# The end of FF2 in a one-layer hybrid decoder step: preloaded residual, a last step in row groups, a norm moved into the next stage

## The chip, the cores and the metric

The kernel runs on one core of one Trainium2 chip. The metric is the device time of one execution in microseconds. PE is the matrix engine, DVE the vector engine, ACT the scalar engine, POOL the general-purpose engine, SP the engine that only issues transfers. PSUM is the memory with eight banks that products are summed in.

## The reference

One layer of a decoder is applied to a prompt of 2048 tokens and to 8 x 4 sampled tokens, with a model width of 1024. Two branches (a gated recurrence and windowed attention) are merged, and an MLP with squared ReLU follows. The part that matters here is the end:

```python
x = x + m @ w_o
h2 = _rmsnorm(x, n2)
x = x + jnp.square(jax.nn.relu(h2 @ w_ff1)) @ w_ff2      # FF1: 1024 -> 4096, FF2: 4096 -> 1024
y = _rmsnorm(x, normf_w)
```

All in float32. `_rmsnorm` divides each token's row by the root of its mean square plus 1e-6 and multiplies by a weight.

## The kernel before

**Layout.** Activations are stored transposed: 128 channels on the partitions, tokens along the free axis. A matrix of 1024 channels is eight tiles (`KD = 8`). The tokens are worked in two superblocks (`sb` 0 and 1) of 1024 and 1056 tokens, each in two halves (`o` 0 and 1) of `Th` = 512 and 528 tokens. In superblock 1 a half doesn't fit one PSUM bank, and is worked in two chunks of 264.

**Products.** Every float32 value is split into a high part, rounded for the fast product format, and a remainder: ACT copies the high part (`split_in`, `split_out`, lines 145 and 249) and DVE subtracts it (lines 146 and 250). A product is then three matmuls: high x high, high x low, low x high (lines 257 to 259 and 1396 to 1398).

**Strassen.** FF1 and FF2 are each done as a 2 x 2 block product by Winograd's form of Strassen, with seven products instead of eight. The blocks are halves of the tokens and halves of the channels. Operands called A11, A12, A22 are blocks, and S1 to S4 are sums of blocks; B.. and T1 to T4 are the same for weights. S operands of FF1 lie in DRAM (`sd`), and so do the operands of FF2, which FF1 writes at its end of each unit (`us`, line 1301, from POOL's queue).

**FF1** (`strassen_T`, `Unit`, `Wpair`) runs in units of one channel tile and one chunk. A unit's part `a` needs only A11, A12 and early weights: two products of 12 matmuls (fB and fC). Six (superblock 0) or ten (superblock 1) units do `a` ahead, with a hook `early(i)` after each, in which the splits of the S operands are done. Then each unit runs `b` (three products) and the unit before it `c` (two products; its last one needs S4).

**FF2** runs the seven steps of the list `steps` one after another. A step takes four groups `g` of 512 of the 4096 channels. For each `g` it loads the operand (`u_load`, line 1351) and two weight blocks (`w2_blk`, line 1335), both from SP's queue, and does 48 products (x 2 chunks) into four PSUM banks, `j` = 0 to 3. After the last `g`, each bank is added to the output blocks that the step belongs to (`evac`, line 1404 for a copy by ACT and line 1406 for an addition by DVE). `yacc` holds the outputs: 16 tiles, eight per half.

The **last step** (A22 x T4) is written out differently. All four groups' operands are loaded first, and the output channels are taken in two pairs (`jp`); for each pair all four groups' weights are held, and each bank runs over all groups before the next begins.

**The final norm** is the class `Fin` inside FF2. `load` brings the residual `x1d` from DRAM (line 1369, SP's queue). `add` adds it to the output (DVE, line 1373), squares it (ACT, line 1374) and sums the squares over channel tiles (POOL, or DVE in the last blocks, line 1378). `end` transposes the sums on PE (line 207), sums on DVE (208), forms the power -1/2 on POOL (210), and spreads the row back over the partitions by transposes on PE (219) and an ACT copy (220). `out` multiplies by weight and norm row (ACT line 1389 and POOL line 1390, or one DVE instruction, line 1387, in the very last tiles) and stores the tile. The first half (`f0`) is normed among the last step's products; the second half (`f1`; two chunks in superblock 1) after them.

**Order.** The code hands instructions to a planner that gives each engine a fixed sequence. The program's order is the priority, and an instruction may move ahead of earlier ones that the planner, by its own costs, thinks not ready. On the chip each engine runs its sequence in order. The lists `todo` and `hooks` decide where in the program order the side work stands: one or two entries are taken after each group of products. The transfers of one issuing engine go out in the order of its sequence too. SRAM tiles of one stage reuse the addresses of earlier stages' tiles and wait for those to be released; `op(slot, ...)` gives seven long-lived slots.

## Time and profile before

| | |
|---|---|
| median of three runs | 2945.36 us (2944.08 to 2948.93) |
| the profiled execution's time | 2943.06 us |
| its span, first to last instruction | 2941.3 us |
| busy share of the span | PE 95%, DVE 60%, ACT 39%, POOL 18% |
| mean granted PE clock | 0.981 |
| first FF2's last step | from 2154.7 us of the span |
| second FF1's first products | from 2211.5 us |
| second FF2's last step, last product | 2856.5, 2926.8 us |

A profile row names a line of the kernel, an engine, the operation and its tiles. "[2.99 <-POOL xo]" behind a row is the time for which the engine stood idle before it, and what ended that. A row of the waits gives the total, the number and the longest. Numbers in tile names are left out, so `f` is any PSUM bank of FF2, `fB_f` and `fC_f` are banks of FF1, `n_y` and `rb_y` are the norm's transposes, and `hw2T`, `lw2T` are the split weights of a T step.

### The profile page before, as it was taken

How to read it: one execution, taken by the hardware profiler on the slowest of the kernel's cores; microseconds unless marked ns; L12 is line 12 of the kernel's file. 1: busy time of each engine (PE TensorE's matmuls, PEld its weight loads, DVE VectorE, ACT ScalarE, POOL GpSimd, SP SyncE). 2: the span in 40 equal slices, each digit the busy share in tenths (PEclk: the TensorE clock that was granted, in tenths of full speed). 3: DMA queues.
4: the chain of work that ended last, by engine and by line, in shares of the span. 5: the costliest groups of instructions: out<-in, count | busy, mean ns of one | idle time of the engine just before them, and what ended most of it. 6: DMA issues, size and time to landing. Idle time of an engine off the chain costs nothing.

```text
span 2941.3 us, 50086 instructions
## 1 busy us (share of the span) xinstructions
PE 2797.4 (95%) x20053; PEld 2438.8 (83%) x20053; DVE 1776.3 (60%) x2785; ACT 1145.0 (39%) x2148; POOL 535.4 (18%) x797
## 2 busy tenths in 40 slices
PE   7999999999999999999999999999986999999996
PEld 5778887787799867777798888778876999999996
DVE  4574645746765367436666877754567777654464
ACT  4442345323444434334333333444443333344342
POOL 0100211102200112320122222100043343300003
PEclk9999999999999999989999999999998999999998
DMA  5227562377633435523355544785555444565553
GB/s 179 74 82 255 192 195 64 96 242 259 222 124 110 131 117 190 172 74 103 107 171 196 183 152 143 262 304 181 200 169 183 156 157 138 168 242 187 192 183 96
DMA packets 347897, 488.81 MB, mean 166 GB/s; under 512 B 22528, under 2 KB 224080, under 8 KB 347648
## 3 DMA queue, kind: packets, MB, share of 16 engines
q1 hardware_dynamic: 295536, 340.84, 37.0%
q0 software_dynamic: 39584, 129.18, 11.9%
q10 hardware_dynamic: 12544, 15.60, 1.5%
q8 instruction: 157, 2.57, 0.4%
...
## 4 chain that ended last, share of the span: by engine, by line
PE 77%; DMA 7%; issue 5%; DVE 5%; POOL 3%; ACT 2%; SPq 0%; DVEq 0%; ACTq 0%; POOLq 0%
PE f L1396 7%; PE f L1397 7%; PE f L1398 7%; PE fB_f L257 3%; PE fB_f L259 3%; PE fB_f L258 3%; PE fD_f L257 2%; PE fD_f L259 2%; PE fD_f L258 2%; PE ps_hgb L159 1%; PE ps_hgb L160 1%; PE wob L1236 1%; PE wob L1234 1%; PE fB_z L257 1%; PE wob L1235 1%
## 5 line engine op out<-in xcount | busy, mean ns | idle before, releaser
L1396 PE MATMUL f<-f2S,hw2T 128*128 128x264 f32 (+1 forms) x576 | 183.6, 319 | 0.0
L1397 PE MATMUL f<-f2S,hw2T 128*128 128x264 f32 (+1 forms) x576 | 183.5, 319 | 0.0
L1398 PE MATMUL f<-f2S,lw2T 128*128 128x264 f32 (+1 forms) x576 | 183.4, 318 | 0.0
L146 DVE TENSOR_TENSOR lw2T<-lw2T,hw2T 128x1024 fp32r<-128x1024 f32 x64 | 83.3, 1304 | 100.2 <-ACT hw2T L145 99.3
L257 PE MATMUL fB_f<-S,w1T_f 128*128 128x264 f32 (+1 forms) x384 | 123.4, 322 | 9.2 <-ACT p_f L320 5.7
L1378 POOL TENSOR_TENSOR xo<-xo 128x512 f32<-128x512 f32 (+2 forms) x25 | 34.3, 1372 | 492.5 <-ACT xo L1374 484.7
L1396 PE MATMUL f<-f2A,h_w2B 128*128 128x264 f32 (+1 forms) x384 | 122.4, 319 | 0.0
L258 PE MATMUL fB_f<-S,w1T_f 128*128 128x264 f32 (+1 forms) x384 | 122.4, 319 | 0.0
L1397 PE MATMUL f<-f2A,h_w2B 128*128 128x264 f32 (+1 forms) x384 | 122.3, 319 | 0.0
L1398 PE MATMUL f<-f2A,l_w2B 128*128 128x264 f32 (+1 forms) x384 | 122.3, 318 | 0.0
L259 PE MATMUL fB_f<-S,w1T_f 128*128 128x264 f32 (+1 forms) x384 | 122.2, 319 | 0.0
L145 ACT CAST hw2T<-lw2T 128x1024 fp32r<-128x1024 f32 x64 | 67.3, 1051 | 134.1 <-DMA lw2T<-w_T 129.9
L1236 PE MATMUL wob<-m_b,l_wob 128*128 128x512 f32 (+2 forms) x320 | 112.3, 352 | 5.3 <-DVE l_wob L250 5.3
L1234 PE MATMUL wob<-m_b,h_wob 128*128 128x512 f32 (+2 forms) x320 | 113.5, 355 | 3.9 <-DVE ga_b L1122 2.8
L1396 PEld LDWEIGHTS f<-f2S,hw2T 128*128 128x128 f32 x576 | 108.4, 188 | 7.5
L1397 PEld LDWEIGHTS f<-f2S,hw2T 128*128 128x128 f32 x576 | 108.4, 188 | 7.4
L1398 PEld LDWEIGHTS f<-f2S,lw2T 128*128 128x128 f32 x576 | 108.0, 188 | 7.5
L1235 PE MATMUL wob<-m_b,h_wob 128*128 128x512 f32 (+2 forms) x320 | 112.5, 352 | 0.0
L146 DVE TENSOR_TENSOR f2S<-f2S 128x1024 fp32r<-128x1024 f32 (+1 forms) x64 | 79.7, 1254 | 48.7 <-ACT f2S L145 48.1
L250 DVE TENSOR_TENSOR l_w2B<-rw2B,h_w2B 128x1024 fp32r<-128x1024 f32 x48 | 58.7, 1224 | 81.8 <-ACT h_w2B L249 72.5
L249 ACT CAST w1T_f<-w1r_f 128x512 fp32r<-128x512 f32 x128 | 77.3, 619 | 79.2 <-DVE w1r_f L293 37.8
L250 DVE TENSOR_TENSOR w1T_f<-w1r_f,w1T_f 128x512 fp32r<-128x512 f32 x128 | 90.1, 710 | 25.8 <-ACT w1T_f L249 25.6
...
## 6 DMA issues: line engine op xcount, KB each, us to landing
...
f2S<-u_S SPq DMA_DIRECT2D x32, 528.0 KB
...
```

Of the source, the lines that this page charges most:

```text
L146: nc.vector.tensor_tensor(lo, F(lo), F(hi), ALU.subtract)
L249: nc.scalar.copy(dh, src)
L250: nc.vector.tensor_tensor(dl, src, F(dh), ALU.subtract)
L257: nc.tensor.matmul(ps, wh, ah, start=(first and k == 0), stop=False, skip_group_check=not first)
L258: nc.tensor.matmul(ps, wh, al, start=False, stop=False, skip_group_check=not first)
L259: nc.tensor.matmul(ps, wl, ah, start=False, stop=(last and k == 3), skip_group_check=not first)
L1234: nc.tensor.matmul(p, wh, ah, start=(k == 0), stop=False)
L1235: nc.tensor.matmul(p, wh, al, start=False, stop=False)
L1236: nc.tensor.matmul(p, wl, ah, start=False, stop=(k == KD - 1))
L1396: nc.tensor.matmul(ps, wh, ah, start=first, stop=False, skip_group_check=cont)
L1397: nc.tensor.matmul(ps, wh, al, start=False, stop=False, skip_group_check=cont)
L1398: nc.tensor.matmul(ps, wl, ah, start=False, stop=lastk, skip_group_check=cont)
```

## The change

- **Residual preload.** In steps 0 to 3 of FF2, after the first group, the residual is loaded from POOL's queue straight into the four output tiles that the step writes first. Every evacuation is then an addition on DVE; the ACT copies, the residual loads on SP's queue and the additions of line 1373 are gone.
- **Last step of superblock 0 by row groups.** It runs in the same loop as the other six. After each of its groups the slot of that group takes the next FF1 operand (S2, S1, S3, A22; loads from POOL's queue); S2 and S1 are split before the stage ends, S3 and A22 in the hooks of FF1.
- **Second half's norm of superblock 0 in the next FF1.** Its output tiles lie in slot 6. Squares, statistics, spread and stores are in the hooks after the first nine units. S4, which needs slot 6, is loaded after the tenth and split in `mid`, after the first `b`.
- **POOL.** The sums of squares and the scalings are DVE instructions. POOL keeps the power and the issue of transfers.
- In superblock 1 the last step keeps its order with two channel pairs; statistics and spread of each norm are entries of their own, some products apart, and the first chunk's norm of the second half is among the last products.
- In the first FF1, the three operand loads stand after unit 0 and their splits after units 3 and 4. Under the w_o product ahead of superblock 1's first stage, the norm of the next tokens is done two channel tiles at a time instead of four.

```diff
                 def fin1(k0, o=o, rbz=rbz, xr=xr):
-                    for k in range(k0, k0 + 4):
+                    for k in range(k0, k0 + 2):
                         norm_x(xr[:, k], k, rbz)
                         if o == 0:
                             split_k(hT_next, k, xr[:, k])
@@ -1220,7 +1225,8 @@
                 half.append((loads, lambda o=o, rbz=rbz: spread(rbz, stats[f"z{o}"].rs, Tn, f"z{o}"), fin1))
             (ld0, rb0_, fin0), (ld1, rb1_, fin1_) = half
-            todo += [ld0, rb0_, lambda: [ld1(), fin0(0)], lambda: [rb1_(), fin0(4)], lambda: fin1_(0), lambda: fin1_(4)]
+            todo += [lambda: [ld0(), rb0_()], lambda: [ld1(), rb1_(), fin0(0)]] + [lambda k=k: fin0(k) for k in (2, 4, 6)]
+            todo += [lambda: [fin1_(0), fin1_(2)], lambda: fin1_(4), lambda: fin1_(6)]
         n2 = Norm(wk_tmp, T, n2c, f"f{B}")
         rings = (sw_ps, mm_ps, hg_ps)
         for n in range(0, KD, 2):
...
+    class Fin:
+        def __init__(f, c0, ln, y, x, ns, q, ring=tp_ps):
+            f.ring, f.c0, f.ln, f.y, f.x, f.ns, f.q, f.acc, f.N = ring, c0, ln, y, x, ns, q, None, f"y{c0}"
+        def sq(f, *js):
+            for j in js:
+                x = f.x("acc" if f.acc is None else "sq")
+                nc.scalar.activation(x, f.y(j), AF.Square)
+                if f.acc is None:
+                    f.acc = x
+                else:
+                    tt(f.acc, f.acc, x, ALU.add)
+        def stat(f):
+            f.rs = f.ns(f"rs_{f.N}")[0:WT[f.ln], 0:f.ln // WT[f.ln]]
+            stat(f.rs, f.acc, f.ln, f.N, f.ring)
+        def spread(f):
+            f.rb = f.x("rb")
+            spread(f.rb, f.rs, f.ln, f.N, f.ring)
+        def out(f, *js):
+            for j in js:
+                y = f.y(j)
+                nc.vector.scalar_tensor_tensor(y, y, nfc[:, j:j + 1], f.rb, ALU.mult, ALU.mult)
+                f.q.dma_start(yT[j * P:(j + 1) * P, f.c0:f.c0 + f.ln], y)
+    f1 = None
     for sb in range(nsb):
         smp, ns, T, segs, halves, tiles = geometry(2 * sb + 1)
         ns2 = ns // 2
         us = {o: [tc.dram_tile([4 * P, Th], F32, name=f"u_{o}_{g}_{sb}") for g in range(KG)] for o in OPS}
         with tc.tile_pool(name=f"f1_{sb}", bufs=1, reuse_waits="tile") as fp:
-            hooks = []
-            for nm, slot in (("S3", 2), ("A22", 3), ("S4", 6)) if sb == 0 else (("S2", 4), ("S1", 5), ("S3", 2), ("A22", 3), ("S4", 6)):
-                ff_ops[nm] = v = opv(slot, nm)
-                hooks += op_load(sb, v, *ff_src(sb, nm), now=False)
+            def get(nm, slot):
+                ff_ops[nm] = opv(slot, nm)
+                return op_load(sb, ff_ops[nm], *ff_src(sb, nm), now=False)
+            if sb == 0:
+                ready = []
+                def split_some():
+                    for _ in range(3):
+                        if ready:
+                            ready.pop(0)()
+                hooks = [[lambda: ready.extend(get("S3", 2) + get("A22", 3) + get("S4", 6))], [], [], [split_some], [split_some], []]
+            else:
+                f1.x = lambda r: fp.tile([P, f1.ln], F32, tag="fa" if r == "acc" else "fs", name=f"fx_{r}")
+                f1.ns = lambda name: fp.tile([P, 8], F32, tag="ns", name=name)
+                hooks = [[lambda: f1.sq(0, 1, 2, 3)], [lambda: f1.sq(4, 5, 6, 7)], late_ops[0:2], [f1.stat], late_ops[2:4], [f1.spread], [lambda: f1.out(0, 1, 2)],
+                         [lambda: f1.out(3, 4, 5)], [lambda: f1.out(6, 7)], [lambda: s4_load.extend(get("S4", 6))]]
+            s4_load = []
             def early(i):
-                for _ in range(2 if i >= (3 if sb == 0 else 4) else 0):
-                    if hooks:
-                        hooks.pop(0)()
+                for f in hooks[i]:
+                    f()
...
         slots = iter([0, 1] + [2, 3, 4, 5] * 8)
         with tc.tile_pool(name=f"f2_{sb}", bufs=1, reuse_waits="tile") as fp:
-            yacc = [[fp.tile([P, Th], F32, tag=f"y{o}{j}", name=f"y{o}{j}_{sb}") for j in range(KD)] for o in range(2)]
-            def y_tmp(tag, name):
+            if last:
+                y1, xo = None, raw8(6, Th, f"xo{sb}")
+            else:
+                y1, xo = raw8(6, Th, f"y1_{sb}"), fp.tile([P, 6, Ths[sb + 1]], F32, name=f"xo{sb}")
+            yacc = [[y1[:, j] if o and not last else fp.tile([P, Th], F32, tag=f"y{o}{j}", name=f"y{o}{j}_{sb}") for j in range(KD)] for o in range(2)]
+            def f2_ns(name):
                 return fp.tile([P, 8], F32, tag="ns", bufs=2, name=name)
+            def fin_of(o, t0, ln, regs, q):
+                regs, n = dict(regs), [0]
+                def x(r):
+                    if r == "sq":
+                        n[0] += 1
+                        r = f"sq{n[0] % 2}"
+                    return xo[:, regs[r], t0:t0 + ln]
+                return Fin(off[sb] + o * Th + t0, ln, lambda j: yacc[o][j][:, t0:t0 + ln], x, f2_ns, q)
...
             def evac(si, j, t0, ln, ps):
                 c11, c12, c21, c22 = (yacc[o][4 * h + j][:, t0:t0 + ln] for o in range(2) for h in range(2))
-                sets, adds = (((c11,), ()), ((c22,), ()), ((c12,), ()), ((c21,), (c22,)), ((), (c11,)), ((), (c12, c22, c21)), ((), (c21,)))[si]
-                for o in sets:
-                    nc.scalar.copy(o, ps)
-                for o in adds:
+                for o in ((c11,), (c22,), (c12,), (c21, c22), (c11,), (c12, c22, c21), (c21,))[si]:
                     tt(o, ps, o, ALU.add)
-            f0 = Fin(0, 0, Th, {**{j: j for j in range(KD)}, "rb": 1})
-            cut = Th // 2 if last else Th
-            f1 = [Fin(1, t0, ln, {4: 2, 5: 3, 6: 4, 7: 5, 0: 6, 1: 7, 2: 3, 3: 4, "rb": 5})
-                  for t0, ln in (((0, cut), (cut, Th - cut)) if last else ((0, Th),))]
+            f0 = fin_of(0, 0, Th, {"acc": 0, "sq0": 1, "sq1": 2, "rb": 3}, nc.gpsimd)
+            cut = Th // 2
+            f1s = [fin_of(1, t0, cut, {"acc": 4, "sq0": 5, "sq1": 6, "rb": 7}, nc.sync) for t0 in (0, cut)]
+            if not last:
+                f1 = Fin(off[sb] + Th, Th, lambda j, y1=y1: y1[:, j], None, None, nc.gpsimd, hg_ps)
+            n_si = 6 if last else 7
             todo = []
-            for si, (ao, wo) in enumerate(steps[:6]):
+            for si, (ao, wo) in enumerate(steps[:n_si]):
                 if fresh[si]:
                     banks = [[rings[si][j](f"f2_{sb}_{si}_{j}_{t0}")[:, 0:ln] for (t0, ln) in chunks] for j in range(4)]
                 if si == 1 and not last:
                     nv = [opT(sb + 1, g, f"A1{g}") for g in range(2)]
-                    rr = raw8(6, Ths[sb + 1], f"fr{sb + 1}")
-                    todo = [lambda k=k: ff_sums(sb + 1, nv, [rr[:, i] for i in range(6)], k) for k in range(4)]
+                    todo = [lambda k=k: ff_sums(sb + 1, nv, [xo[:, i] for i in range(6)], k) for k in range(4)]
+                    todo = [f for t in todo for f in (none, none, none, t, none, none, none, none)]
                     ff_ops = {"A11": nv[0], "A12": nv[1]}
                 if si == 5:
-                    xo = raw8(6, Th, f"xo{sb}")
-                    todo += [lambda: [f0.load(j) for j in range(4)], lambda: [f0.load(j) for j in range(4, 8)],
-                             lambda: [f0.add(0), f0.add(1)], lambda: [f0.add(2), f0.add(3)]]
+                    todo += [none] * 8 + [lambda: f0.sq(0), lambda: f0.sq(1), lambda: f0.sq(2), lambda: f0.sq(3)]
+                elif si == 6:
+                    todo = [lambda: f0.sq(4, 5), lambda: f0.sq(6, 7), none, f0.stat, none, none, f0.spread] + [lambda j=j: f0.out(j) for j in range(KD)]
+                    late_ops = []
                 for g in range(KG):
                     av = u_load(ao, g)
                     wb = [w2_blk(wo, 4 * g + 2 * h, 2, 0, 512, f"{sb}{g}{h}") for h in range(2)]
                         if g == KG - 1:
                             for ci, (t0, ln) in enumerate(chunks):
                                 evac(si, j, t0, ln, banks[j][ci])
-                    if todo and (si == 5 or g % 2):
-                        todo.pop(0)()
+                        if todo:
+                            todo.pop(0)()
+                    if g == 0 and si < 4:
+                        o, h = ((0, 0), (1, 1), (0, 1), (1, 0))[si]
+                        for j in range(4 * h, 4 * h + 4):
+                            nc.gpsimd.dma_start(yacc[o][j], x1d[sb][j * P:(j + 1) * P, o * Th:(o + 1) * Th])
+                    if si == 6:
+                        for f in late_ops[0:2] if g >= 2 else []:
+                            f()
+                        late_ops = late_ops[2:] if g >= 2 else late_ops
+                        nm = ("S2", "S1", "S3", "A22")[g]
+                        ff_ops[nm] = opT(sb + 1, (4, 5, 2, 3)[g], nm)
+                        late_ops += op_load(sb + 1, ff_ops[nm], *ff_src(sb + 1, nm), now=False)
             while todo:
                 todo.pop(0)()
+            if not last:
+                continue
             ao, wo = steps[6]
             avs = [u_load(ao, g) for g in range(KG)]
-            def none():
-                pass
-            def each(fn, *js):
-                return lambda: [getattr(f, fn)(j) for f in f1 for j in js]
-            todo = [lambda j=j: f0.add(j) for j in range(4, KD)]
-            todo = todo[2:] + [each("load", 0, 1)] + todo[:2] + [each("load", 4, 5, 6, 7), none, none, none, f0.end]
-            outs = [lambda j=j: f0.out(j) for j in range(KD)]
-            todo += [each("add", 4), outs[0], each("add", 5), outs[1], each("add", 6), each("load", 2, 3), each("add", 7)] + outs[2:]
+            todo = [lambda: f0.sq(4), lambda: f0.sq(5), lambda: f0.sq(6), lambda: f0.sq(7), none, none, f0.stat, none, none, none, f0.spread]
+            todo += [lambda j=j: f0.out(j) for j in range(KD)] + [lambda j=j: [f.sq(j) for f in f1s] for j in range(4, KD)]
+            end0 = [none, none, none, f1s[0].stat, none, f1s[0].spread, lambda: f1s[0].out(0, 1, 2, 3), lambda: f1s[0].out(4, 5, 6, 7)]
             for jp in range(2):
                 wts = []
                 for g in range(KG):
                     wts.append(w2_blk(wo, 4 * g, 4, jp * 256, 256, f"{sb}{g}_{jp}"))
-                for f in f1:
+                for fi, f in enumerate(f1s):
+                    t0 = fi * cut
                     for j in range(2):
                         js = slice(j * P, (j + 1) * P)
-                        ps = rings[6][2 * jp + j](f"f2_{sb}_6_{jp}{j}_{f.t0}")[:, 0:f.ln]
+                        ps = rings[6][2 * jp + j](f"f2_{sb}_6_{jp}{j}_{t0}")[:, 0:cut]
                         for g in range(KG):
                             for k in range(4):
-                                gemm2(ps, wts[g][0][:, k, js], wts[g][1][:, k, js], avs[g], f.t0, f.ln, k, g == 0 and k == 0, g == KG - 1 and k == 3)
-                            for _ in range(1 if last else 2):
-                                if todo:
-                                    todo.pop(0)()
-                        evac(6, 2 * jp + j, f.t0, f.ln, ps)
-                        f.add(2 * jp + j, nc.vector)
-                    if jp == 1:
-                        while todo:
-                            todo.pop(0)()
-                        f.end()
-                        for j in range(KD):
-                            f.out(j, last and j < 6)
+                                gemm2(ps, wts[g][0][:, k, js], wts[g][1][:, k, js], avs[g], t0, cut, k, g == 0 and k == 0, g == KG - 1 and k == 3)
+                            if todo:
+                                todo.pop(0)()
+                        evac(6, 2 * jp + j, t0, cut, ps)
+                        f.sq(2 * jp + j)
+                    if jp == 1 and fi == 0:
+                        todo += end0
+            while todo:
+                todo.pop(0)()
+            f1s[1].stat()
+            f1s[1].spread()
+            f1s[1].out(*range(KD))
```

53 lines of the change are left out of this document (16 added, 37 removed).

## The prediction

> **What bounds the kernel now.** I read the share of busy time first (PE 95% of the span), so only stretches where PE stops can give much. I found them in the view of PE's waits, and then cut the span there. Columns of the stretches: length, then busy time (instructions) of PE, PEld, DVE, ACT, POOL, then granted PE clock, DMA share, GB/s.
>
> ```profile
> 2154.70:2211.60 56.90, 47.98 (x202) 39.17 (x201) 40.91 (x38) 25.96 (x37) 32.67 (x31) 0.91 0.56 179
> 2211.60:2259.00 47.40, 24.66 (x156) 23.12 (x155) 36.85 (x39) 17.52 (x28) 22.11 (x25) 0.78 0.57 196
> 2259.00:2560.00 301.00, 298.72 (x2424) 295.74 (x2423) 216.47 (x468) 105.73 (x231) 108.95 (x204) 1.00 0.45 146
> ...
> 2856.40:2927.00 70.60, 55.83 (x404) 53.78 (x403) 39.06 (x61) 20.04 (x36) 27.82 (x23) 0.88 0.36 114
> 2927.00:2941.30 14.30, 1.27 (x6) 0.71 (x6) 5.47 (x11) 0.80 (x2) 2.47 (x3) 0.58 0.22 76
> ```
>
> These are, in order: the last step of the first FF2 (A), the first products of the second FF1 (B), a normal stretch for comparison, the last step of the second FF2 (C), the end after the last product (D). The undisturbed rates:
>
> ```profile
> 2000.00:2025.00 25.00, 25.00 (x112) 20.71 (x111) 11.79 (x10) 11.20 (x13) 0.00 (x0) 1.00 0.55 176
> ...
> 2425.00:2450.00 25.00, 25.00 (x208) 25.00 (x208) 18.41 (x39) 10.05 (x22) 9.23 (x18) 1.00 0.44 148
> ```
>
> A 512-column product takes 25.00/112 = 0.223 us, a 264-column one 25.00/208 = 0.120. A has 192 products (42.9 us at that rate) and takes 56.9: **14.0 lost**. B holds 156 instructions (18.8 us) and takes 47.4: **28.6 lost**. C has 384 (46.2) and takes 70.6: **24.4 lost**. D is 14.3 of pure tail. Together 81 us that are not products. Who holds PE there:
>
> ```profile
> PE rb_y L219 <- POOL rs_y L210: 15.0, 4, 6.6
> PE fC_f L257 <- DVE p_f L335: 8.8, 4, 6.4
> PE n_y L207 <- DVE xo L1378: 8.0, 2, 6.0
> PE f L1396 <- ACT hw2T L145: 6.4, 1, 6.4
> ...
> PE fB_f L257 <- ACT p_f L320: 5.7, 1, 5.7
> PE wob L1236 <- DVE l_wob L250: 5.3, 2, 2.8
> ...
> PE f L1396 <- ACT y L1404: 2.9, 1, 2.9
> ```
>
> The norm's transposes (n_y, rb_y) stand in PE's order ahead of products that were ready, and wait for a chain over DVE, ACT and POOL:
>
> ```profile
> 2171.48 1.12 PE L207 MATMUL n_y<-ident,xo 128*128 128x128 f32 x4 [2.99 <-POOL xo L1378]
> 2172.24 0.78 PE L1396 MATMUL f<-f2A,hw2T 128*128 128x512 f32 x1
> ...
> 2181.90 1.11 PE L219 MATMUL rb_y<-ident,rs_y 128*128 128x128 f32 x4 [5.93 <-POOL rs_y L210]
> ...
> 2217.19 0.39 PE L257 MATMUL fB_f<-A,w1B_f 128*128 128x264 f32 x1 [2.60 <-DVE y L1406]
> ...
> 2225.45 1.08 PE L207 MATMUL n_y<-ident,xo 128*128 128x128 f32 x4 [6.03 <-DVE xo L1378]
> ...
> 2882.47 1.14 PE L219 MATMUL rb_y<-ident,rs_y 88*128 88x88 f32 x6 [6.58 <-POOL rs_y L210]
> ...
> 2903.35 0.59 PE L1396 MATMUL f<-f2A,hw2T 128*128 128x264 f32 x1 [6.42 <-ACT hw2T L145]
> ```
>
> **The change, part by part.**
>
> POOL without sums and scalings. While POOL multiplies y by the norm row, DVE's additions stretch fivefold:
>
> ```profile
> 2236.07 3.60 DVE L293 TENSOR_TENSOR w1r_f<-w1r_f,w1r_f 128x512 f32<-128x512 f32 x1
> ...
> 2260.75 0.68 DVE L293 TENSOR_TENSOR w1r_f<-w1r_f,w1r_f 128x512 f32<-128x512 f32 x1
> 2236.63 2.48 POOL L1390 TENSOR_TENSOR y<-y,xo 128x512 f32<-128x512 f32 x2
> ```
>
> DVE is 36.9 of 47.4 us busy in B because of this, and the fC_f and fB_f waits (6.4 and 5.7) follow. DVE now does the scalings as one instruction each (0.60 to 0.68 us) and the sums at 0.68; the code moves 28 scalings and 25 sums to it, some 33 us over stages where it is half idle.
>
> A: the norm of the first half has no residual additions in front. Its statistics are placed after the first of four row groups (10.7 us in) and the spread three blocks of 12 products later, 3 x 12 x 0.223 = 8.0 us. The chain between them, when DVE is not stretched, is this (sum, power, copy of the spread row):
>
> ```profile
> 2226.57 0.69 DVE L208 TENSOR_REDUCE rs_y<-n_y 128x4 f32<-128x512 f32 x1
> 2228.60 1.96 POOL L210 TENSOR_TENSOR rs_y<-rs_y,negh 128x4 f32<-128x4 f32 x1 [15.19 <-DVE rs_y L209]
> 2231.36 0.59 ACT L220 COPY xo<-rb_y 128x512 f32<-128x512 f32 x1 [2.41 <-PE rb_y L219]
> ```
>
> From the transposes' end (2225.45 + 1.08) to the end of the power 4.0 us, less than 8.0. So A = 42.9 + 1.5 for two groups of transposes (1.12 and 1.11, less their overlap with products) + 1.5 for what I can't see = 45.9: **-11.0**. Bounds of the unseen wait: 0 and the 5.93 of today.
>
> B: the second half's norm leaves the seam and its squares, with a single buffer, run among ten units of 24 products (2.9 us each). The output rows moved to a tile that outlives the stage, so new tiles no longer wait for it. POOL's queue holds the four operand loads, each behind its row group on PE, then the second half's outs, then S4's load, which waits for these outs to land. Behind the first operand load stands the norm's power, due at about the time that row group ends; behind S4 stand only stores of u, for which no product waits soon. Losses I put in: transposes 1.2; statistics late 2, because eight squares and seven sums are one chain and the statistics stand after unit 3 (11.6 us); spread late 1 (5.8 us of room against 4.0); DVE work 3; S4 late 1; slow clock 2.
>
> ```profile
> L1374 ACT ACTIVATE xo<-y 128x512 f32<-128x512 f32 x12 | 7.5, 631 | 10.2 <-DVE y L1373 10.1
> ...
> L146 DVE TENSOR_TENSOR S<-S 128x1056 fp32r<-128x1056 f32 x8 | 9.9, 1253 | 4.1 <-ACT S L145 4.1
> ```
>
> The squares chain is 8 x (0.63 + 0.68 + 0.1) = 11.3 us. DVE's work over the ten units is 20 evacuations and products' ends at 0.43, ten weight splits at 0.68 (four done earlier), the sums 4.8, four operand splits at 1.25, statistics 0.9, scalings 5.4, the next pair's weights 5.4: about 34 us against PE's 28.9 + 1.2, hence 3 (bounds 0 and 5). S4:
>
> ```profile
> S<-dS POOLq DMA_DIRECT2D x8, 528.0 KB, 6.7
> out_yT<-y POOLq DMA_DIRECT2D x16, 256.0 KB, 2.8
> ```
>
> last scaling at about 29, landing 2.8, S4 6.7, cast and split 2.3: ready at 41; PE reaches it at 28.9 + 1.2 + 5.8 (48 products) plus its own delays, 36 to 42. Bounds 0 and 5. In sum B loses 10.2 instead of 28.6: **-18.4** (bounds -27 and -8). The Trainium skill ("TensorE: Matmul & The Clock Gate", section "HAM oscillation") lets only idle gaps above some 3.4 us drop the clock. The trace shows slow products (0.78 for 0.39) already after 2.99 us and none after 2.60. By that page my 2 us of slow clock would vanish and B would be 2 better.
>
> C: the order of products stays, but the residual loads leave SP's queue. Today the last weights stand behind them:
>
> ```profile
> 2887.89 0.38 SPq L1335 DMA_DIRECT2D lw2T<-w_T  x1
> 2892.93 3.31 SPq L1369 DMA_DIRECT2D xo<-x1d  x2
> 2896.30 0.42 SPq L1392 DMA_DIRECT2D out_yT<-y  x1
> 2896.82 0.38 SPq L1335 DMA_DIRECT2D lw2T<-w_T  x1
> ```
>
> Their buffer came free 1.4 us after that of the load at 2887.89, so they start some 7 us earlier; the 6.42 becomes 0 to 2.5, I take 1. The spread stands 4 x 12 x 0.120 = 5.8 us after the statistics, so the 6.58 goes too. C = 46.2 + 2.0 (four groups of transposes) + 1 + 1.2 (small waits as now) = 50.4: **-20.2** (bounds -23 and -12).
>
> D: per last block one residual addition less (0.47 with its hop), two scalings more on DVE (3.58/6 = 0.60 each). And the first half's eight scalings are listed at the last two groups of products, ahead of the last evacuation on DVE: they can start 1.9 us before the last product's end and take 4.8, so the evacuation is 2.9 late.
>
> ```profile
> 2927.34 0.43 DVE L1373 TENSOR_TENSOR y<-y,xo 128x264 f32<-128x264 f32 x1
> ...
> 2932.45 3.58 DVE L1387 SCALAR_TENSOR_TENSOR y<-y,cols,xo 128x264 f32<-128x264 f32 x6 [2.25 <-ACT xo L220]
> ```
>
> **+3.6** (bounds +0.7 and +5.5).
>
> E: sixteen preloads per FF2 on POOL's queue (behind the last stores of u, and behind the release of the y tiles; the last row group's evacuation of each of steps 0 to 3 waits for them), and evacuations that were ACT copies become DVE additions (0.43 to 0.68, hidden while DVE is half idle). The loads may all start at the stage's head, where DMA is full:
>
> ```profile
> 1875.00:1900.00 25.00, 22.50 (x100) 18.31 (x99) 22.77 (x28) 12.20 (x13) 5.41 (x10) 1.00 0.97 361
> ```
> ```profile
> xo<-x1d SPq DMA_DIRECT2D x6, 256.0 KB
> ```
>
> 16 x 0.262 MB = 4.2 MB at 361 GB/s is 11.6 us if all of it delays weights, 0 if none; the same bytes come early today as well. I take 1.5 per stage: **+3** (bounds 0 and 23).
>
> F: norm work of the next block in smaller pieces under w_o. The 5.3 us of wob waits stand behind runs of four norms on DVE: **-3** (bounds -5.3 and +5.3). The load order ahead of the first FF1: 0.
>
> Sum: -11.0 - 18.4 - 20.2 + 3.6 + 3 - 3 = -46.0. From the profiled execution (span 2941.3, time 2943.06) that is 2897.1; the median of the runs is 2.3 above that execution, so I say **2899**.
>
> **Rivals.** (1) The transposes wait as they do now, only elsewhere: 2.99 + 5.93 + 6.03 + 6.58 = 21.5, some 5 of slow clock, (the clock of A and C is 0.91 and 0.88), less the 4.5 I have in: 22 back, 2921. For it: PE is in order, and five such pairs remain. Against: statistics and spread are now apart. (2) Preloads starve the weights: 11.6 + 11.9 in place of 3, 2919. The Trainium skill says the same from its side ("DMA: Bandwidth & Descriptors", section "Queues, rings and completion order"): an engine takes turns between queues, so a full POOL queue takes half from SP's; by it the 11.6 per stage stands. The trace has no such mix at a stage's head. (3) Everything fits: B loses only 1.2, D +0.7, F -5.3, E 0, C's wait 0: 19 more, 2880. (4) B gains nothing, because the squares and scalings merely fill the place: 2917. (5) **Slower**: the evacuations of steps 0 to 5 now stand in DVE's order behind splits that wait for weights, and PE may not go on in the same banks before them. It happened once, on ACT: the 2.9 us row above, behind a weight load of this length:
>
> ```profile
> 1968.69 8.55 DMA rw2B<-w_ff
> ```
>
> There are twelve such boundaries. At 5.7 us each (the mean of the two) that is 68 against 46: 2967; it decides from 46/12 = 3.8 us. Against it: the steps that already evacuate by DVE additions show no wait of PE.
>
> **How the numbers follow.** Chances: forecast 0.51 (own range 2884 to 2914), (1) 0.14, (2) 0.12, (3) 0.13, (4) 0.05, (5) 0.05. Range 2880 to 2932 leaves out (5) and half of (3), with some of the edges. A measurement of this kernel can tell about 0.2% (6 us) from no change. Faster: all but (5) and the far tails, 0.93; within 0.02; slower 0.05.
>
> **What would show it.** In the changed profile: A near 46 us with no rb_y wait above 2; B's first ten units without a gap above 3 us and no DVE addition of 3 us; no hw2T wait in C; the last evacuation some 3 us after the last product; the heads of both FF2 no worse than now. A rb_y or n_y row above 5 us speaks for (1), a longer first step of FF2 for (2), waits of the f products for DVE y at step boundaries for (5).

## The result and the profile after

| | before | after |
|---|---|---|
| median of four runs each, us | 2945.25 (2944.08 to 2948.93) | 2895.45 (2894.06 to 2902.43) |
| ratio, with its 95% interval | | 0.9834 (0.9815 to 0.9852) |
| the profiled execution, us | 2943.06 | 2894.51 |
| its span, us | 2941.3 | 2892.7 |
| predicted, us | | 2899 (2880 to 2932) |

The change makes the kernel 1.7% faster, 3.6 us below the predicted time. First, the stretches of the profile after that answer to those of the prediction: A, B, a normal stretch, C and D, with the same columns (length, busy time and count of PE, PEld, DVE, ACT, POOL, then granted PE clock, DMA share, GB/s).

```profile
2150.10:2194.50 44.40, 44.40 (x200) 36.47 (x199) 31.07 (x38) 18.19 (x23) 9.77 (x15) 1.00 0.72 239
2194.50:2242.00 47.50, 40.10 (x313) 39.66 (x313) 39.29 (x70) 19.91 (x39) 15.21 (x24) 0.95 0.58 196
2242.00:2547.50 305.50, 296.87 (x2375) 293.27 (x2374) 216.66 (x463) 108.81 (x232) 110.96 (x207) 0.99 0.47 153
2827.70:2880.10 52.40, 50.07 (x402) 48.57 (x401) 33.62 (x61) 13.77 (x24) 6.76 (x10) 1.00 0.32 108
2880.10:2892.70 12.60, 1.41 (x6) 0.74 (x6) 5.59 (x14) 0.80 (x2) 0.84 (x1) 0.59 0.43 146
```

A has no idle PE and a full clock: 44.4 us instead of 56.9. C is 52.4 instead of 70.6, its clock 1.00 instead of 0.88. D is 12.6 instead of 14.3. B still has idle time: 47.5 us that hold 313 products and transposes, where before the same time held 156. At 0.120 us each these are 37.6, so 9.9 are lost, and about 1 more in slow products up to 2245: some 11 instead of 28.6. The stretch behind it, up to the end of the second FF1, has 8.6 us without a product (305.50 less 296.87). The normal stretch of the prediction had 2.3, but it ended at 2560, ahead of a wait; up to the stage's end (2575.5) it is 4.6 in the kernel before. The view of PE's waits over the whole kernel shows what is left (total, number, longest, in us):

```profile
PE fB_f L257 <- ACT c_f L320: 9.2, 4, 4.9
...
PE fB_f L257 <- DVE c_f L322: 3.0, 2, 1.7
...
PE fB_f L257 <- DVE y L1436: 2.1, 1, 2.1
...
PE rb_y L219 <- POOL rs_y L210: 1.9, 1, 1.9
```

The rb_y waits were 15.0 in four; one of 1.9 is left, in the tail. The fC_f waits of 8.8 are gone from the head of the list. Two waits of fB_f for DVE's c_f (1.2 and 1.7) stand behind B, at 2273.75 and 2311.63. The one new long wait is fB_f behind ACT's c_f copy, 4.9 us. It lies in B, from 2233.51 us on, and the timelines of POOL (the first three rows) and ACT at that place show how it comes about:

```profile
2218.41 2.53 POOL L1292 DMA_DIRECT2D out_yT<-y  x4
...
2224.07 0.54 POOL L1292 DMA_DIRECT2D out_yT<-y  x1 [0.46 <-DVE y L1291]
...
2231.17 1.45 POOL L564 DMA_DIRECT2D S<-dS  x2 [3.73 <-DMA out_yT<-y]
...
2235.48 1.07 ACT L145 CAST S<-S 128x1056 fp32r<-128x1056 f32 x1 [5.92 <-DMA S<-dS]
...
2236.98 1.07 ACT L145 CAST S<-S 128x1056 fp32r<-128x1056 f32 x1
2237.95 0.37 ACT L320 COPY c_f<-fB_f 128x264 f32<-128x264 f32 x1
```

S4 takes the slot of the second half's rows, so its load on POOL's queue waits until the eight rows have landed, the last issued at 2224.07. ACT has the cast of S4 next in its fixed order and stands idle for 5.92 us; the copy that PE needs to go on stands behind it. These are PE's two stretches right after that gap:

```profile
2238.40:2241.40 3.00, 3.00 (x14) 3.00 (x15) 3.00 (x6) 0.00 (x0) 0.20 (x1) 0.50 0.00 0
2241.40:2244.40 3.00, 3.00 (x16) 3.00 (x16) 1.48 (x4) 2.12 (x5) 0.89 (x2) 0.54 0.25 87
```

Six microseconds at a clock of 0.50 to 0.54: the gap costs about 3 us more than its own length. The tail's DVE rows:

```profile
2877.55 3.32 DVE L1291 SCALAR_TENSOR_TENSOR y<-y,cols,xo 128x264 f32<-128x264 f32 x8 [2.46 <-ACT xo L220]
2880.79 0.43 DVE L1436 TENSOR_TENSOR y<-f,y 128x264 f32<-128x264 f32 x1
...
2886.08 3.32 DVE L1291 SCALAR_TENSOR_TENSOR y<-y,cols,xo 128x264 f32<-128x264 f32 x8 [2.23 <-ACT xo L220]
```

Eight scalings take 3.32 us, 0.415 each, where before six took 3.58. The last evacuation starts at 2880.79, 0.74 us after the last product's end (2880.05).

Stage by stage, from the first and last products in PE's timeline of each profiled execution (the second FF1 runs from the last product of the first FF2 to the first of the second; the tail from the last product to the end of the span), with all experiments below, in us:

| kernel | start of first FF1 | first FF2 | second FF1 | second FF2 | tail | median of runs |
|---|---|---|---|---|---|---|
| before | 1570.6 | 322.8 | 363.8 | 351.4 | 14.4 | 2945.25 |
| after | 1565.2 | 312.0 | 352.9 | 332.6 | 12.7 | 2895.45 |
| e5, after again | 1564.5 | 312.6 | 347.4 | 332.7 | 12.5 | 2890.15 |
| e1, scalings on POOL | 1564.2 | 314.0 | 351.8 | 337.9 | 14.0 | 2900.14 |
| e2, no distance | 1560.4 | 312.5 | 349.5 | 336.0 | 11.5 | 2887.51 |
| e3, norm at the seam | 1563.9 | 312.0 | 343.7 | 332.7 | 12.5 | 2884.49 |
| e10, e3 again | 1568.9 | 312.0 | 343.3 | 333.3 | 12.3 | 2889.66 (one run) |
| e4, c later | 1558.1 | 310.5 | 344.7 | 333.4 | 12.5 | 2881.41 |
| e9, rows earlier | 1559.9 | 312.0 | 346.6 | 331.8 | 12.5 | 2882.64 |
| e6, before with sums on DVE | 1572.0 | 321.9 | 365.2 | 347.9 | 14.4 | 2928.43 |
| e7, norm by four | 1564.6 | 312.6 | 351.4 | 332.6 | 12.5 | 2893.47 |
| e8, preloads twice | 1563.7 | 312.4 | 347.3 | 336.7 | 12.5 | 2892.47 |
| e11, column pairs | 1563.7 | 314.4 | 349.3 | 333.5 | 12.5 | 2898.80 |
| e12, before, tail on DVE | 1567.3 | 322.9 | 366.2 | 350.1 | 12.6 | 2938.05 (one run) |

The start of the first FF1 differs by 10 us among executions of kernels that are alike up to there (1558.1 to 1568.9), and the kernel before had medians of 2941.4 to 2945.3 in the four comparisons. So a small effect is read from the stage that the edit touches, not from the median alone.

### The profile page after: what moved, and what is told of

It reads as the page before. It is cut to its first block, busy times and chain, and to the rows that moved or that the text cites. A ratio compares the mean times of both kernels' runs of the same rounds, so it can differ in the third digit from the quotient of the medians.

```text
span 2892.7 us, 49998 instructions
## 1 busy us (share of the span) xinstructions
PE 2783.1 (96%) x20053; PEld 2427.2 (84%) x20053; DVE 1768.6 (61%) x2846; ACT 1111.0 (38%) x2072; POOL 486.2 (17%) x784
## 4 chain that ended last, share of the span: by engine, by line
PE 79%; DMA 6%; issue 5%; DVE 5%; POOL 2%; ACT 2%; SPq 0%; POOLq 0%; DVEq 0%; ACTq 0%
PE f L1431 6%; PE f L1430 6%; PE f L1429 6%; PE fB_f L257 4%; PE fB_f L259 3%; PE fB_f L258 3%; PE fD_f L257 2%; PE fD_f L259 2%; PE fD_f L258 2%; PE wob L1241 1%; PE wob L1240 1%; PE wob L1242 1%; PE fB_z L257 1%; PE fB_z L259 1%; PE fB_z L258 1%
## 5 line engine op out<-in xcount | busy, mean ns | idle before, releaser
L1429 PEld LDWEIGHTS f<-f2S,hw2T 128*128 128x128 f32 x576 | 108.8, 189 | 10.9 <-ACT hw2T L145 3.5
L1356 POOL DMA_DIRECT2D u_S<-s_f x144 | 77.7, 541 | 114.8 <-DVE s_f L1351 91.7
L1356 POOL DMA_DIRECT2D u_A<-c_f x106 | 57.4, 542 | 233.2 <-DVE c_f L1340 232.0
```

Of the source, the lines that this page charges most:

```text
L1356: nc.gpsimd.dma_start(us[o][u.n // 4][u.n % 4 * P:(u.n % 4 + 1) * P, u.t0:u.t0 + u.ln], y_)
L1429: nc.tensor.matmul(ps, wh, ah, start=first, stop=False, skip_group_check=cont)
```

## The experiments

The theory behind the prediction was: the waits went because statistics and spread were set apart, because the norm has work beside it, and because POOL no longer stretches DVE. Each experiment undoes one of these, or tries one alone.

**Scalings back on POOL (e1).**

```diff
-nc.vector.scalar_tensor_tensor(y, y, nfc[:, j:j + 1], f.rb, ALU.mult, ALU.mult)
+nc.scalar.activation(y, y, AF.Copy, scale=nfc[:, j:j + 1])
+nc.gpsimd.tensor_tensor(y, y, f.rb, ALU.mult)
```

> The norm's scalings go back to ACT (copy with a scale) and POOL (product with the norm row), everywhere where the changed kernel does them on DVE in one instruction (0.41 to 0.68 us each). Theory (POOL's products stretch DVE's work beside them, as the 3.60 us additions of the kernel before): DVE additions of 2 to 3.6 us are back among the first products of the second FF1, the second half's rows leave later there, S4's load too, and the gap ahead of fB_f grows from 4.9 to some 10 us; the tail's eight scalings take 5 us instead of 3.3. Together 8 to 15 us slower than the changed kernel, 2903 to 2911. Rival (DVE is full in that stretch and POOL idle, so that any work taken from DVE helps): 0 to 5 us faster, 2890 to 2895.

Measured: 2900.14 us, ratio 0.9856 (0.9834 to 0.9878); below the theory's 2903 and above the rival's 2895. Timelines of POOL, then DVE, in B:

```profile
2223.79 2.54 POOL L1292 TENSOR_TENSOR y<-y,fx_rb 128x512 f32<-128x512 f32 x2
...
2227.39 2.51 POOL L1292 TENSOR_TENSOR y<-y,fx_rb 128x512 f32<-128x512 f32 x2
...
2221.48 0.42 DVE L335 TENSOR_TENSOR c_f<-fC_f,p_f 128x264 f32<-128x264 f32 x1
...
2223.18 3.44 DVE L1341 SCALAR_TENSOR_TENSOR c_f<-c_f 128x264 f32<-128x264 f32 x1
2226.55 0.68 DVE L293 TENSOR_TENSOR w1r_f<-w1r_f,w1r_f 128x512 f32<-128x512 f32 x1
2227.26 3.20 DVE L294 TENSOR_TENSOR w1r_f<-w1r_f 128x512 f32<-128x512 f32 x1
```

The stretch is back: a DVE instruction that takes 0.42 or 0.68 us alone lasts until a pair of POOL's products is over (DVE to 2226.62, POOL to 2226.33; then 2230.46 against 2229.90). The Trainium skill ("SBUF — State Buffer", section "Who interferes with whom") says that a DVE instruction with two SBUF inputs and one of POOL that reads SBUF contend for one pair of ports, and that this pair is an exclusive lock. The ends of these rows agree; that DVE's first row began 0.6 us ahead of POOL's pair and was held off all the same is not explained by it. It doesn't always fall on DVE alone: in the pair of products before, POOL took 4.12 us (2218.59 to 2222.71) instead of 2.5, and DVE's rows there at most 1.50. PE waits 6.3 us once for a c_f listed behind such rows; the fB_f gap of 4.9 us is not there. The second FF1 (351.8) lies between the two executions of the changed kernel (352.9 and 347.4), so whether the rows cost anything there is not shown. The cost that is clear lies elsewhere: the second FF2 is 5.3 us longer, the tail 1.3. In the second FF2's last step PE waits 5.0 us for weight splits of DVE (2.0 in the changed kernel):

```profile
PE f L1432 <- DVE lw2T L146: 5.0, 3, 2.7
```

So the stretch is shown and costs, but not, as far as can be told, in B, the place that the theory named for it.

**No distance between statistics and spread (e2).**

```diff
 def stat(f):
     stat(f.rs, f.acc, f.ln, f.N, f.ring)
+    f.rb = f.x("rb")
+    spread(f.rb, f.rs, f.ln, f.N, f.ring)
 def spread(f):
-    f.rb = f.x("rb")
-    spread(f.rb, f.rs, f.ln, f.N, f.ring)
+    pass
```

> The transposes that spread the norm row follow those of the statistics at once on PE, with no products between. Theory (the distance is what removed the rb_y waits): four pairs lose it (one in A, one in B, two in C), each waits for the chain of sum, power and hop, 4.0 us at 512 columns and some 3.5 at 264: 15 us, and 3 to 5 us of slow clock behind them: 18 to 20 us slower, 2913 to 2916, with rb_y waits of 3.5 to 6 us. Rival (the waits went because POOL no longer stretches the chain, and the distance adds little): rb_y waits under 2 us, at most 6 us slower, below 2902.

Measured: 2887.51 us, 0.9809 (0.9787 to 0.9832). The theory's 2913 to 2916 is excluded; the rival holds, but for one wait above its 2 us. Rows of POOL and PE in A, then PE's rb_y waits in A and B, and in C:

```profile
2157.36 1.04 POOL L210 TENSOR_TENSOR rs_y<-rs_y,negh 128x4 f32<-128x4 f32 x1 [1.42 <-DVE rs_y L209]
...
2154.77 0.60 PE L207 MATMUL n_y<-ident,xo 128*128 128x128 f32 x4
...
2158.45 0.65 PE L219 MATMUL rb_y<-ident,rs_y 128*128 128x128 f32 x4 [1.47 <-POOL rs_y L210]
```
```profile
PE rb_y L219 <- POOL rs_y L210: 4.7, 2, 3.2
...
PE rb_y L219 <- POOL rs_y L210: 2.2, 2, 1.4
```

In A and B they are 1.47 and 3.23, in C 1.36 and 0.82: 6.9 us in four, not 15. From the end of the statistics' transposes (2155.37) to rb_y it is 3.1 us, and the planner puts seven products into it by itself. In the kernel before, the same way took 9.3 us (2172.59 to 2181.90). What stood in it can be read there, in DVE's timeline and then in POOL's:

```profile
2175.36 0.68 DVE L208 TENSOR_REDUCE rs_y<-n_y 128x4 f32<-128x512 f32 x1
...
2177.32 1.23 DVE L209 TENSOR_SCALAR rs_y<-rs_y 128x4 f32<-128x4 f32 x1
```
```profile
2175.58 4.29 POOL L1378 TENSOR_TENSOR xo<-xo 128x512 f32<-128x512 f32 x3 [4.16 <-ACT xo L1374]
2179.82 2.03 POOL L210 TENSOR_TENSOR rs_y<-rs_y,negh 128x4 f32<-128x4 f32 x1
```

The power (L210) stood in POOL's order behind three sums of squares of other rows, without an idle moment ahead of it, and took 2.03 us where it takes 1.04 above. Of the 6.2 us between 9.3 and 3.1, 1.2 are that place in POOL's order and 1.0 the longer power. The other 4.0 lie ahead of it, on DVE: L208 starts 2.8 us after the transposes, behind an evacuation, a weight split and two additions of the residual, instead of 1.0; and L209, with one more residual addition between, ends 3.2 us after that start instead of 0.9. So DVE's residual additions and POOL's queue, not only the place of the transposes, made the wait.

The distance does help: counted by products, the last step of the first FF2 is 1.7 us longer without it (46.3 and 44.6) and that of the second 2.3 (54.8 and 52.5). In B nothing can be told: the S4 gap falls to 2.5 us, a rb_y wait of 3.2 comes in, and the second FF1 (349.5) lies between the changed kernel's two executions.

**The kernel before, with only its sums on DVE (e6).** This tests that reading from the other side.

```diff
-def add(f, j, eng=nc.gpsimd):
+def add(f, j, eng=nc.vector):
```

> The kernel before with one edit: the sums of squares are all on DVE (0.68 us each), not on POOL (1.4 us each); scalings, places and order stay. Theory (the rb_y waits of 5.93 and 6.58 us came from the power standing in POOL's order behind three and more of POOL's sums, 4.3 and 3.4 us in one row each): both waits fall under 3 us, and with the slow clock behind them this alone makes the kernel before 8 to 14 us faster, 2931 to 2937. Rival (the chain was long because POOL's work stretches DVE's, or because the transposes stand too near): a wait is only exchanged for later DVE work, 0 to 4 us faster, 2941 to 2945.

Measured: 2928.43 us (ten runs, 2922.74 to 2937.76), 0.9956 (0.9941 to 0.9971): 13 us faster than the kernel before, within the theory's 8 to 14. PE's waits in A and B, then in C:

```profile
PE n_y L207 <- DVE xo L1378: 4.5, 2, 3.4
...
PE rb_y L219 <- POOL rs_y L210: 3.4, 1, 3.4
```
```profile
PE rb_y L219 <- POOL rs_y L210: 4.1, 2, 3.5
PE f L1396 <- ACT hw2T L145: 3.2, 2, 2.8
```

The waits of 5.93 and 6.58 fall to 3.4 and 3.5, a little above the 3 expected, and n_y's in B from 6.0 to 3.4. The hw2T wait of C falls from 6.42 to 2.8 too, though the residual loads are still ahead of the weights. The profiled execution is the slowest of the ten and shows only 3.0 us less in the three stages together. By steps, the two last steps are 5.0 and 3.5 us shorter; longer are the second FF1 (1.4) and the earlier steps of the first FF2 (4.1, with a wait of 4.5 us for an ACT copy, L1404, that is 2.9 us in the kernel before). So the profile shows what the waits gave, 8.5 us, and not where all of the 13 us went.

**The norm back at the seam (e3, and again e10).** Squares of rows 4 to 7 among the last row group, the rest after the last product; the hooks keep only S3's and A22's splits and S4's load.

```diff
             while todo:
                 todo.pop(0)()
             if not last:
+                f1.sq(0, 1, 2, 3)
+                f1.stat()
+                f1.spread()
+                f1.out(*range(KD))
                 continue
```

> The second half's norm of the first column block is back at the end of the first FF2, ahead of the second FF1's products: squares of rows 4 to 7 among the last row group's products, of rows 0 to 3 behind the last products, statistics, spread and scalings at once. Theory (the place among the first products is what gained in B): PE waits at the seam some 5 us for the four squares and sums, 4 for the norm row, and some 3 of slow clock behind, while B's first products lose the 4.9 us gap ahead of fB_f with its 2 us of slow clock, since the rows leave earlier: 5 to 10 us slower, 2900 to 2905. Rival (POOL's release of DVE made the gain in B, and the place is worth nothing): within 3 us of 2895, or faster, since the 4.9 us gap goes.

> The kernel of e3_norm_at_seam again, on this chip, for its stages beside the next ones and the control: if its lead was its own, the second FF1 takes 343 to 345 us with about 6 us of waits at the seam and no wait over 1.5 us at fB_f; if it was the execution's, 347 or more.

Measured: 2884.49 us, 0.9807 (0.9783 to 0.9831); in e10 one run of 2889.66. The second FF1 takes 343.7 and 343.3 us, against 352.9 and 347.4 of the changed kernel: the rival holds. PE's waits in B of e3:

```profile
PE fB_f L257 <- DVE y L1433: 2.7, 1, 2.7
PE fB_f L257 <- ACT c_f L320: 1.8, 2, 1.4
PE rb_y L219 <- POOL rs_y L210: 1.8, 1, 1.8
PE n_y L207 <- DVE xo L1278: 1.5, 1, 1.5
```

The seam costs 6.0 us in three waits (2.7, 1.5, 1.8) with no slow clock in B (its granted clock is 1.00, not 0.95; in e10 it is 0.50 for 3.4 us behind the first of them), and the 4.9 us gap is down to 1.4. So the place among the first products is not needed for the shorter B; with POOL out of the way the norm is short enough to stand at the seam, and the later place delays S4.

**The first unit's last products later (e4), the rows earlier (e9).**

```diff
+swap = free and nch > 1 and i == 1
-if i:
+if i and not swap:
     units[i - 1].c()
 ...
 u.b()
-if i == 0:
+if i == (nch > 1):
     mid()
+if swap:
+    units[0].c()
```

> In the second FF1 the second unit's three middle products (36 products of 0.12 us, 4.3 us) go ahead of the first unit's last ones, and the cast and split of S4 are listed behind them on ACT and DVE. Theory (the 4.86 us gap ahead of fB_f is ACT standing on S4's load in order, ahead of a copy that PE needs): that gap shrinks to under 1.5 us and the slow clock behind it goes, 4 to 7 us faster than the changed kernel, 2888 to 2891. Rival (DVE is full there and PE would wait for it a little later anyway): gaps of the same sum between 2230 and 2260 us, 0 to 2 us faster, 2893 to 2895.

> The edit of e4_c_later, and the second half's norm row is spread after unit 4 instead of 5, its rows leave after units 5 to 7, and S4 is loaded after unit 8 (each one unit, 2.9 us, earlier). Theory (what is left of B's loss is S4's arrival, with ACT standing on it in order): the gap ahead of fB_f, 4.9 us in the changed kernel and 3.4 in e4, falls under 1 us, and the second FF1 takes 341 to 343 us (control 347.4, e4 344.7). Rival (the row isn't ready earlier, PE waits at rb_y instead, or DVE is late next): 344 us or more.

Measured: e4 2881.41 us, 0.9803 (0.9778 to 0.9828), second FF1 344.7; e9 2882.64, 0.9803 (0.9787 to 0.9819), second FF1 346.6. ACT's timeline of e4, then PE's waits of e9 in B and its two stretches after the S4 gap:

```profile
2230.15 1.07 ACT L145 CAST S<-S 128x1056 fp32r<-128x1056 f32 x1 [5.63 <-DMA S<-dS]
...
2232.62 0.65 ACT L320 COPY c_f<-fB_f 128x264 f32<-128x264 f32 x2
```
```profile
PE fB_f L257 <- ACT c_f L320: 3.6, 2, 2.5
...
PE rb_y L219 <- POOL rs_y L210: 1.2, 1, 1.2
```
```profile
2232.70:2235.70 3.00, 2.97 (x14) 2.97 (x15) 3.00 (x4) 1.62 (x3) 0.00 (x0) 0.55 0.00 0
2235.70:2238.70 3.00, 3.00 (x24) 3.00 (x23) 3.00 (x7) 1.46 (x4) 0.45 (x1) 0.88 0.00 0
```

In e4 the gap shrinks only from 4.9 to 3.4 us, not under the 1.5 expected, since the planner still lists the cast ahead of copies that PE needs, and the slow clock behind it stays (0.50 for 6.8 us). The waits in the first 125 us of the stage, apart from the very first, halve (5.1 us, against 10.5 in after and 9.6 in the control), and the stage is 2.7 us shorter than the control's, 8.2 than that of after. In e9 the gap shrinks to 2.5, but 1.2 us of rb_y wait comes in and DVE is full behind it (3.00 of 3.00 in both stretches): its rival holds. Both kernels stand at 0.9803, against 0.9834 and 0.9823 for the changed kernel's two comparisons. The intervals overlap, so a lead of some 0.25% is likely from the stage and not established by the medians.

**Control (e5).** The changed kernel again, beside e6 to e8.

> The changed kernel itself again, beside the next three, since the stages ahead of every edit differed by up to 7 us between executions so far. If those differences belong to the execution, its median lies anywhere from 2885 to 2900 and its stages from the start of the first FF2 on repeat within 3 us: first FF2 312, second FF1 353 with a gap of 4 to 5 us ahead of fB_f, second FF2 333, tail 12.6. If the lead of the two kernels with 2884 and 2881 us was the chip's and not their edit's, the second FF1 here takes 344 to 346 us.

Measured: 2890.15 us, 0.9823 (0.9802 to 0.9844). Both FF2 and the tail repeat within 0.6 us. The second FF1 takes 347.4 instead of 352.9, with the same S4 gap (4.8), so this stage varies by 5.5 us between two executions, more than the 3 expected.

**Norm pieces of four again (e7).** The list of work under w_o is put back as in the diff's removed lines.

> Under w_o ahead of superblock 1's first stage the norm of the next tokens is done four channel tiles at a time again, from the same places as in the kernel before. Theory (the smaller pieces made the second w_o stage shorter): that stage takes 53 to 55 us instead of 49.3, the 3.5 us wait behind it (rb_fb, 768 us) goes, and the sum to the start of the first FF1 is 0 to 5 us more than in the control of the same call. Rival (the lead of 5.3 us that the changed kernel had at the first FF1 is the execution's, not the edit's): the stage takes 53 to 55 us and the start of the first FF1 lies within 2 us of the control's, or ahead of it.

Measured: 2893.47 us, 0.9844 (0.9817 to 0.9872). Under w_o and shortly after, PE's waits of the control, then of e7:

```profile
PE rb_fb L219 <- POOL rs_fb L210: 3.5, 1, 3.5
PE wob L1242 <- DVE l_wob L250: 2.8, 2, 1.7
```
```profile
PE wob L1241 <- DVE l_wob L250: 5.3, 2, 2.8
```

The stage takes 53.8 us instead of 49.2, but the small pieces pay 3.5 of it back right after. At the first FF1 the two kernels stand at 1564.6 and 1564.5: the rival holds. As e7 has the kernel before's order of instructions on every engine up to there, and yet starts the first FF1 6.0 us earlier than it, the 5.3 us by which after led before at that point are not shown to come from the edit.

**Preloads twice (e8).**

```diff
 nc.gpsimd.dma_start(yacc[o][j], x1d[sb][...])
+nc.gpsimd.dma_start(yacc[o][j], x1d[sb][...])
```

> Each of the 32 residual preloads of the two FF2 is issued twice: 4.2 MB more per FF2 on POOL's queue, nothing else. Theory (the preloads run in time that the weights leave free): each FF2 within 2 us of the control's, together 0 to 4 us slower. Rival (preloads take the weights' share): 4.2 MB at 361 GB/s is 11.6 us per FF2, 15 to 23 us slower, with waits of the f products for weights in steps 0 to 3.

Measured: 2892.47 us, 0.9829 (0.9806 to 0.9852). The first FF2's first 50 us, e8 and control:

```profile
1878.90:1928.90 50.00, 50.00 (x222) 41.42 (x221) 28.18 (x33) 15.49 (x18) 22.62 (x42) 1.00 1.01 376
```
```profile
1879.50:1929.50 50.00, 50.00 (x222) 41.43 (x221) 29.64 (x36) 15.95 (x19) 16.67 (x31) 1.00 0.94 333
```

DMA is full, and PE has no idle time in either: weights are far enough ahead. The stages grow by -0.2 and 4.0 us, not by 11.6 each. The 4.0 don't lie where the preloads run: counted by products, the steps 0 to 5 take 267.8 and 280.9 us here, 267.9 and 280.7 in the control. The second FF2's last step, which issues no preload, takes 55.8 instead of 52.0, with a wait of 2.6 us for hw2T and a slow clock behind it. So the rival falls, and the cost of the doubled preloads is within the noise.

**Column pairs in the first FF2's last step (e11).** The loop of superblock 1's last step, with 512 columns, replaces the row groups; the four operand loads follow it.

> The last step of the first FF2 runs by column pairs again, as in the kernel before, with the norm at the same distances in products as in the changed kernel; so the four operands of the second FF1 (S2, S1, S3, A22) can be loaded only at the end of the stage, and all eight splits fall among the first products. Theory (the row groups matter for B, by freeing the operand slots, and not for A): the first FF2 stays at 311 to 314 us, the second FF1 is 5 to 10 us longer than the control's 347.4, since DVE is full there and eight splits of 1.25 us are four more than now. Rival (the row groups themselves made A shorter): the first FF2 takes 317 us or more, the second FF1 347 to 350.

Measured: 2898.80 us, 0.9855 (0.9839 to 0.9871). The first FF2 is 314.4 us, 0.4 above the theory's range and below the rival's; the second FF1 349.3, only 1.9 above the control, as the rival had it and not the theory's 5 to 10. The likely reason is that the operands' loads now meet the weights of the first products. PE's first wait in B, and ACT's row behind it, which waits for such a weight:

```profile
PE fB_f L257 <- DVE y L1436: 7.8, 1, 7.8
```
```profile
2204.67 0.62 ACT L249 CAST w1B_f<-w1r_f 128x512 fp32r<-128x512 f32 x1 [5.36 <-DMA w1r_f<-w_ff]
```

The 7.8 us wait is one that the row groups remove; the S4 gap is smaller here (3.1), so the stage shows less of it. The row groups are worth about 4 us in these two stages, by this pair of executions; by the medians the kernel is 8.7 us slower than the control without them, and where the rest lies is not shown.

**The kernel before, tail scalings all on DVE (e12).**

```diff
-f.out(j, last and j < 6)
+f.out(j, last)
```

> The kernel before, with all eight scalings of each last half on DVE instead of six (the other two were ACT and POOL). Theory (the 0.60 us of one scaling in the tail was 0.42 stretched by POOL's products beside it): eight take 3.3 to 3.4 us, against 3.58 for six, and from the last product to the end 14.0 to 14.4 us, as before or shorter. Rival (0.60 us is the price of a 264-column scaling): eight take 4.8 us and the tail 15.2 to 15.7.

Measured: the tail is 12.6 us, below the theory's 14.0 to 14.4. DVE's row for it:

```profile
2929.58 3.32 DVE L1387 SCALAR_TENSOR_TENSOR y<-y,cols,xo 128x264 f32<-128x264 f32 x8 [2.25 <-ACT xo L220]
```

Eight take 3.32 us without POOL's products; six beside two of these took 3.58 (the prediction's row). That settles the price. But most of the 1.9 us by which this tail is shorter lies behind the scalings: from their end to the end of the span it is 5.2 us in the kernel before (2936.03 to 2941.28) and 3.4 here (2932.90 to 2936.28). What the end waited for there stands in the view of the program's closing line (L1547) of the kernel before, among rows of the engines' sequencers (count, then the shortest, median and longest in ns):

```profile
L1547 POOLq DRAIN  x3: 40/102/8042, 2932.5 to 2941.0; - x3
```

POOL's first closing DRAIN begins at 2932.46 beside its last products, which end at 2934.12, and lasts until 2940.50. SP's last closing instruction ahead of it ends at 2938.85, so the end waits 1.7 us for POOL alone. In e12 POOL's ends ahead of SP's (2934.7 and 2935.5). Why it lasts 6.4 us beyond the last product, where in e1 it is 1.0 behind eight of them, is not shown.

## Why the prediction was right, and where not

| term | predicted | profile after less before | experiments |
|---|---|---|---|
| A | -11.0 | -12.5 (56.9 to 44.4) | distance worth 1.7 (e2), POOL's sums 5.0 (e6) |
| B | -18.4 | -17.5 (28.6 to 11.1 lost) | -18.2 in the control (10.4 lost) |
| second FF1 behind B | 0 | +6.6 (-10.9 for the stage, less B) | +1.9 in the control |
| C | -20.2 | -18.2 (70.6 to 52.4) | distance worth 2.3 (e2), POOL's sums 3.5 (e6) |
| D | +3.6 | -1.8 | -1.9 with eight scalings on DVE alone (e12) |
| E | +3 | +1.0 (rest of both FF2: +1.6, -0.6) | doubled: -0.1 and +0.2 in the steps that preload (e8) |
| F | -3 | -5.3 at the first FF1, with what else varies there | 0 at that point (e7) |
| first FF1 | 0 | -0.9 | |
| sum | -46.0 | -48.6 | |

**The sum** was right, and A, B and C, nearly all of it, to within 2 us each. Two errors cancel, by luck: D was 5.4 us too gloomy, and 6.6 us behind B weren't in the prediction at all. What the residual preload gained is not measured apart: no run puts the residual additions back.

**A and C** came out at the forecast's size and for half of its reason. The step that failed is the reading that the transposes' place made the rb_y waits, and that the 8.0 us of products behind the statistics cover the chain of 4.0. The chain had been long since DVE's residual additions stood in it and the power stood behind POOL's sums (9.3 us; e6, which frees it of the sums alone, takes 2.5 and 3.1 us off the two waits); freed of both, it takes 3.1 us in A, and PE waits 0.8 to 3.2 for it without any distance (e2). Rival 1 (2921) priced these waits with the chain of before, 21.5 us; with all distance taken away they were 6.9, and the kernel's median was no slower. The prediction quoted the POOL row of 2228.60, where POOL was idle ahead of the power, and missed the row of 2179.82, where it wasn't. The reason given for C's hw2T wait, the residual loads on SP's queue, is in part wrong too: with these loads in place it fell by 3.6 of 6.4 in e6.

**B:** the sum of its losses held (10.2 and 11.1), its parts did not. The failed step is "S4 late 1" with "slow clock 2": S4 cost 4.9 and the clock 3. Counted from B's first product (2196.62), the prediction had S4 ready at 41 and PE there at 36 to 42. S4's second cast ended at 2238.05, 41.4 after that product, and PE stopped at 2233.51, at 36.9: the 1 stood for a PE that would be delayed on the way, and it came almost undelayed. Parts of the 41 were off and cancelled: the rows' landing was 5.6 us (median of eight sent in a burst) rather than 2.8, S4's load 4.5 rather than 6.7, and the last row left at 27.5 rather than 29. What PE waited for was not S4 itself but a copy behind its cast in ACT's order. Against this the statistics were late by 0.5 and not 2, the spread not at all, and DVE's work cost 2.1 (the first fB_f) and not 3.

**Behind B** the prediction had nothing. In the first 70 us after it there are five waits, 5.2 us together (4.2 in the control), of which the fB_f rows for DVE's c_f are the larger part; in the kernel before they are under 1. At the stage's end there is a gap of 2.9 us (2.6 in the kernel before, 1.7 in the control), and of these three only after has the slow clock behind it: 0.50 for 6.8 us, some 3 us of loss. So the 6.6 are 4.0 of gaps (8.6 against 4.6) and that slow clock. Why DVE is late behind B stays open: it stood idle in the S4 gap (6.7 us ahead of S4's split), but in e4 it stood idle for 6.8, and the stage behind 2243 has 3.9 us of gaps there, not 8.6.

**The clock** fell to 0.50 after the 4.86 us gap, about 3 us of loss. The Trainium skill ("TensorE: Matmul & The Clock Gate", section "HAM oscillation") puts the bound at gaps above some 3.4 us. Here the clock also fell after gaps of 2.55 us (e9, 0.55 in the row above) and 2.94 (after, among the last products of the second FF1, the row below), and in the first FF2 even after 1.87 (after, 0.50 from 1954.0 to 1957.4) and 1.81 (e3, 0.50 from 1950.4 to 1953.8); it did not after one of 2.72 (e3, 2191.15 to 2193.87). So gaps shorter than the page's bound cost too, and length alone doesn't divide them.

```profile
2531.60:2534.60 3.00, 2.96 (x13) 2.96 (x14) 0.97 (x1) 0.00 (x0) 0.00 (x0) 0.50 0.58 163
```

**D:** the failed step is the price of 0.60 us for a scaling. It came from a row during which POOL multiplied too, and the prediction had itself shown what POOL's products do to DVE's rows. At 0.415 the first half's eight let the last evacuation start 0.74 us after the last product and not 2.9, and the last eight take 3.32 instead of 4.8. Up to the last scaling's end the tail is then 0.2 longer than before (9.35 and 9.19 us), and 1.9 shorter behind it (3.3 and 5.2), which no term held: 1.7 of it is POOL's closing DRAIN (e12).

**E:** the cost of 3 was right within 2 us, if the rest of both FF2 is put down to it, and rival 2 (2919) fell with e8: twice the bytes cost nothing that can be seen in the steps that preload, not 23. **F:** the waits under w_o went as forecast, and were paid back at rb_fb.

**Rivals 3, 4 and 5.** Everything fits (2880) needed B without loss (its parts come to 18.2 us, not the 19 that the prediction says). B gains nothing (2917) is excluded by the 17.5 us. The slower case (2967) would show f products waiting for DVE y at step boundaries; there is no such row among PE's waits of the whole kernel. Of the signs named, rb_y without a wait above 2, no DVE addition of 3 us and no hw2T wait of weight in C came as said; "B without a gap above 3 us" failed, and the last evacuation was 0.7 late, not 3.
